# A hybrid attention and pooling layer on one core: the second layer norm, the forget logits, the loads of later heads and the output-weight splits, each put in another place

## The chip, the cores and the metric

The kernel runs on one core of a Trainium2 chip. The metric is device time in microseconds (us), the median of several runs. Five engines have a queue of their own and meet only through semaphores: PE (TensorE, matmuls), DVE (VectorE), ACT (ScalarE), POOL (GpSimd) and SP (SyncE). In this kernel SP issues every DMA.

## What is computed

One decoder layer on 2064 tokens (16 learned meta tokens ahead of 2048) of width 1024, in float32. Cut to what matters here:

```python
h = layer_norm(concat([meta, x]), ln_in_g, ln_in_b)
q, k, v, f_logit, g_att, u, g_pool = split(h @ w_in)        # 16 heads of 64
log_f = log_sigmoid(f_logit + b_forget); c = cumsum(log_f)
s = q.k / 8 + c_q - c_k                                     # causal
a = softmax(s) @ v * silu(g_att)
p = multiscale_pool(u) @ w_pool * pool_scale * silu(g_pool)
y = concat([a, p]) @ w_out
out = layer_norm(2 ** 0.25 * h + y, ln_g, ln_b)[:, 16:]
```

## The kernel before, in words

Every matrix operand is kept as two parts, a high part (`wh`, `hh`, `ph`: a copy rounded to the format that PE reads) and a low part (`wl`, `hl`, `pl`: the original less the high part). A product is then three matmuls (high x high, high x low, low x high; `mm3`, L107). `split` (L112) makes the parts: ACT copies, then DVE (or POOL) subtracts. A wrapper (L65 to L88) records every instruction and chains PE, DVE, ACT and POOL each to the order in which the code is written, so the trace gives L86 as the line of nearly everything, and tiles have to be told by name. SP is not chained: the tile scheduler places the DMAs.

The program has four stages.

1. **Input norm and values (0 to 232 us).** The tokens are worked in 17 tiles of 128 rows. `ln_norm(i)` (L227) takes the statistics of a tile's rows on DVE (`bn_stats`, `bn_aggr`), the root on ACT, the reciprocal and the shift on DVE, applies them on ACT, and multiplies by the gain `g_bc` and adds the shift `b_bc`, on the engines it is given (POOL by default). `ln_turn(i)` (L248) transposes the tile on PE (`tr`) and splits it into `hh` and `hl`. `v_tile(0, wts, i, each)` (L280) multiplies tile i by the first half of the value weights in eight steps of three matmuls, and calls `each(k)` after step k; the loop at L341 uses this to put `ln_turn(i + 1)` behind step 3 of tile i. The weights `wvh`, `wvl` of that half are split on ACT and DVE at L320 to L337, between the first norms. Then comes the second half of the values.
2. **Fused pool weights (232 to 262 us).** `fuse_mm(g)` (L418) multiplies the weights of the pool input by those of pool group g, for four groups: 48 matmuls of 256 columns each into two `fz` banks. `fuse_load`, `fuse_split` and `fuse_out` (L433 to L466) load and split a group's weights and write the result to DRAM (`wupd`). The code at L468 to L484 interleaves them. Then the forget logits (L507): five chunks of 16 matmuls into `d`, which has two banks; ACT copies one half of a chunk out (`zc`), DVE adds the other half, and a DMA writes it to `fd`.
3. **Projections (to 1316 us).** Queries and keys, gates and pool, with row maxima of the scores between them (`mx`).
4. **Attention and output (1316 us to the end).** The scores are worked in units: one key tile of 128 against a block of 512 queries, `(head, j)`, with 3, 7, 11 or 15 units in a block, so 36 to a head. A unit is two matmuls into `s` (four banks), two exponentials on ACT (`ph` and, in place, `s`), `pl = s - ph` on DVE (`emit_pl`), and, `LAG` = 4 units later, matmuls into `xo` and `yo`. The output projection runs as a filler: `fill(k)` puts up to four of its matmuls (`d<-wh,xm`) into a unit, from unit 24 on. Its weights come by `wo_task` (L941): `service()` (L1255), called in every second unit, is a round; each round first runs what is due (`todo_late`), then starts one load of 256 KB into `wst` (four buffers); the split of that load falls due three rounds later. There are three such sets of eight weights, at the start of attention, in the middle and near its end. `prefetch` (L888), called in every unit, takes the next group of 512 keys and values (`ka`, `kb`, `vt`) off a queue: any one group a call, and beyond that those that the current block or the next needs (`near`). Heads two apart share buffers, so a head's first group cannot be loaded before the head two before it is done. Phase C, the second norm of the output, follows.

Of the kernel before, what the change touches and what calls it, by code (L numbers as in the profile page):

```python
# [9 lines left out]
F32 = mybir.dt.float32  # L10
# [6 lines left out]
P = 128  # L17
# [18 lines left out]
def f32(ap):  # L36
    return ap.bitcast(F32)
# [3 lines left out]
def kernel(  # L41
# [59 lines left out]
    def dma(out, in_):  # L101
        out, in_ = out[tuple(slice(None) for _ in out.shape)], in_[tuple(slice(None) for _ in in_.shape)]
        nc.sync.dma_start(
            out.bitcast(F32) if out.dtype == F32R else out, in_.bitcast(F32) if in_.dtype == F32R else in_
        )
# [69 lines left out]
    def dense():  # L175
        return psd.tile([P, 512], F32, tag="d", name="d", bufs=2)
# [18 lines left out]
    with ExitStack() as vscope:  # L195
# [19 lines left out]
        def rows_of(i):  # L215
            return min(P, L - P * i)
# [7 lines left out]
            dma(xt[lo:n], x[P * i + lo - NM : P * i + n - NM, :])  # L224
            xts[i] = xt

        def ln_norm(i, engs=None):  # L227
            n = rows_of(i)
            xt = xts[i]
            st = lnp.tile([P, 2, 6], F32, tag="bst", name="bst", bufs=2)  # L230
            for k in range(2):
                nc.vector.bn_stats(out=st[:n, k, :], in_=xt[:n, 512 * k : 512 * (k + 1)])
            mv = lnp.tile([P, 2], F32, tag="mv", name="mv", bufs=2)
            nc.vector.bn_aggr(out=mv[:n], in_=st[:n])
            rs = lnp.tile([P, 1], F32, tag="rs", name="rs", bufs=2)
            nc.scalar.activation(out=rs[:n], in_=mv[:n, 1:2], func=AF.Sqrt, bias=eps_t[:n])
            nc.vector.reciprocal(rs[:n], rs[:n])
            nb = lnp.tile([P, 1], F32, tag="nb", name="nb", bufs=2)
            nc.vector.scalar_tensor_tensor(
                out=nb[:n], in0=mv[:n, 0:1], scalar=-1.0, in1=rs[:n], op0=ALU.mult, op1=ALU.mult  # L240
            )
            nc.scalar.activation(
                out=xt[:n], in_=xt[:n], func=AF.Identity, scale=rs[:n], bias=nb[:n]
            )
            for op, row, eng in zip((ALU.mult, ALU.add), (g_bc, b_bc), engs or (nc.gpsimd, nc.gpsimd)):
                eng.tensor_tensor(out=xt[:n], in0=xt[:n], in1=row[:n], op=op)

        def ln_turn(i):  # L248
            n = rows_of(i)
# [17 lines left out]
        def wv_split(st):  # L267
            h_, l_ = wslot("wvh"), wslot("wvl")
            split(h_, l_, st)
            return h_, l_  # L270
# [9 lines left out]
        def v_tile(half, wts, kt, each):  # L280
            ps = dense()
            sl = slice(P * kt, P * (kt + 1))
            for k in range(KT):
                mm3(ps, hh[:, k, sl], hl[:, k, sl], wts[k][0], wts[k][1], k == 0, k == KT - 1)
                each(k)
            v_out(half, kt, P, ps)
# [33 lines left out]
        def wv_hi(k):  # L320
            nc.scalar.copy(out=wts[k][0], in_=raw[k])
# [9 lines left out]
            wv_lo(k)  # L331
        ln_turn(0)
        ln_load(3)
        for k in range(2, KT):
            if k > 2:
                wv_hi(k)
            wv_lo(k)  # L337
        ln_norm(1, both)
        ln_norm(2, (nc.vector, nc.gpsimd))

        for i in range(NKT - 1):  # L341
            if 4 <= i + 4 < NKT:
                ln_load(i + 4)
            if i + 3 < NKT:
                ln_norm(i + 3)
            if i == 2:
                dma(wfs, wf)
                dma(bf_t, b_forget)
                dma(psc_t, pool_scale)
            if i == 5:  # L350
                split(wfr[:, :, 0:H], wfr[:, :, 32 : 32 + H], wfs)
            if i == 14:
                sts = deque(wv_load(1, k) for k in range(3))

            def turn(k, i=i):
                if k == 3:
                    ln_turn(i + 1)

            v_tile(0, wts, i, turn)
        w1 = [wv_split(sts.popleft())]  # L360
        lnscope.close()
        wq = pool(phase_a, "wq", side="right")
# [70 lines left out]
        def fuse_out(g, made):  # L433
            os = []
            for ps in made:
                os.append(raw4())
                nc.scalar.copy(out=os[-1], in_=ps)
            for half, o in enumerate(os):
                o = o.rearrange("p (k b e) -> p k b e", k=4, b=2)
                for b in range(2):  # L440
                    dma(wupd[2 * g + b][:, 4 * half : 4 * half + 4, :], o[:, :, b, :])
# [13 lines left out]
        def fuse_split(g, r):  # L455
            wst, st = r
            slots = []
            for k in range(2):
                if g % 2:
                    slots.append([fz.tile([P, D], F32R, tag=t, name=t, bufs=2) for t in ("uh", "ul")])  # L460
                else:
                    slots.append([flat(t) for t in w_slots()])
            us[g].append(u_split(st[0], slots[0]))
            wps[g] = [fz.tile([P, 2, 256], F32R, tag=t, name=t, bufs=2) for t in ("ph", "pl")]
            split(*wps[g], halves(wst))
            us[g].append(u_split(st[1], slots[1]))  # L466
# [5 lines left out]
        fuse_split(1, r)  # L472
        r = fuse_load(2)
        fuse_out(0, made)
        fuse_split(2, r)
        made = fuse_mm(1)
        r = fuse_load(3)
# [26 lines left out]
    )  # L504
    ones = fp.tile([P, 1], F32, tag="ones", name="ones")
    nc.vector.memset(ones, 1.0)
    for c0, c1 in CHUNKS:  # L507
        n = c1 - c0
        ps = dense()
        for k in range(KT):  # L510
            mm(ps[:48, :n], wfr[:, k, :], hh[:, k, c0:c1], start=k == 0, stop=False)
            mm(ps[:48, :n], wfr[:, k, :], hl[:, k, c0:c1], start=False, stop=k == KT - 1)
        zc = f32(qp.tile([P, 416], F32R, tag="lo", name="zc", bufs=2))[:H]
        nc.scalar.activation(
            out=zc[:, :n], in_=ps[32 : 32 + H, :n], func=AF.Identity, bias=bf_t
        )
        nc.vector.tensor_tensor(out=zc[:, :n], in0=ps[:H, :n], in1=zc[:, :n], op=ALU.add)
        dma(fd[:, c0:c1], zc[:, :n])
    FW = L // 8
    zf = fp.tile([P, FW], F32, tag="zf", name="zf")  # L520
    dma(zf, fd.rearrange("h (s t) -> (h s) t", s=8))
# [362 lines left out]
        kvq.extend((h, i) for i in range(4) if i <= j and (h, i) not in kvq)  # L884
    fetched = [0]
    cornered = [0]

    def prefetch(n, nv):  # L888

        k = 0  # L890
        while kvq:
            h, i = kvq[0]
            near = any(t[0] == h and t[1] >= i for t in seqn[n : n + 2])
            if h >= 2 and last_use[h - 2] >= nv or (k and not near) or first_use[h] > n + 5:
                break
            load_kv(h, i)
            kvq.popleft()
            k += 1
        while fetched[0] < min(NB, n + 3):
            load_q(fetched[0])  # L900
            fetched[0] += 1
        if cornered[0] < H and first_use[cornered[0]] <= n + 3:
            load_corner(cornered[0])
            cornered[0] += 1
# [36 lines left out]
    def wo_task(args):  # L941
        def a():
            st = wo_load(bw, *args)
            todo_late.append((state["round"] + 3, lambda: wo_split(bw, *args, st, None)))

        return a

# [505 lines left out]
```

## Time and profile before

| | |
|---|---|
| median of 3 runs | 2349.0 us (2347.35 to 2353.8) |
| the profiled execution | 2348.34 us, its span 2346.6 us |
| busy, share of the span | PE 97%, DVE 62%, ACT 42%, POOL 33% |
| DMA | 335.41 MB, mean 143 GB/s |

A profile's row of a timeline gives the start in us, the duration in us, the engine, the line, the operation, output<-inputs, and in brackets how long the engine had been idle and what it waited for. Rows of the chain of waits give start, duration and what the end of the program hung on then. A row of the windows gives, for a stretch of the span, its length and for each engine the busy time and the count of instructions, then the granted TensorE clock (1.00 is full speed) and the DMA share. A wait of PE costs time; a wait of another engine costs time only if PE comes to wait for it.

### The profile page before, as it was taken

How to read it: one execution, taken by the hardware profiler on the slowest of the kernel's cores; microseconds unless marked ns; L12 is line 12 of the kernel's file. 1: busy time of each engine (PE TensorE's matmuls, PEld its weight loads, DVE VectorE, ACT ScalarE, POOL GpSimd, SP SyncE). 2: the span in 40 equal slices, each digit the busy share in tenths (PEclk: the TensorE clock that was granted, in tenths of full speed). 3: DMA queues.
4: the chain of work that ended last, by engine and by line, in shares of the span. 5: the costliest groups of instructions: out<-in, count | busy, mean ns of one | idle time of the engine just before them, and what ended most of it. 6: DMA issues, size and time to landing. Idle time of an engine off the chain costs nothing.

```text
span 2346.6 us, 32233 instructions
## 1 busy us (share of the span) xinstructions
PE 2266.2 (97%) x11146; PEld 1902.4 (81%) x11146; DVE 1464.9 (62%) x2360; ACT 978.3 (42%) x1895; POOL 783.6 (33%) x624
## 2 busy tenths in 40 slices
PE   6999999999999999999999799999999999999998
PEld 4878799999999999999888577777777777776787
DVE  5521246755766567656634388787878777767347
ACT  4421421222212212211111387878878877776000
POOL 4700021222313404140010146555565655545000
PEclk9999999999999999999999899999999999999999
DMA  6743532222222222222222766675767767555955
GB/s 228 226 140 105 154 97 63 91 65 85 89 63 91 82 72 85 62 96 81 80 69 70 194 188 195 192 212 171 201 193 200 207 194 222 167 163 178 290 186 168
DMA packets 347778, 335.41 MB, mean 143 GB/s; under 512 B 57888, under 2 KB 271344, under 8 KB 347584
## 3 DMA queue, kind: packets, MB, share of 16 engines
q1 hardware_dynamic: 347616, 333.37, 47.0%
q8 instruction: 88, 1.44, 0.3%
q14 instruction: 74, 0.61, 0.1%
HBM read 209.15 MB, written 124.13 MB: 142 GB/s over the span
## 4 chain that ended last, share of the span: by engine, by line
PE 90%; DVE 3%; DMA 2%; issue 2%; ACT 2%; POOL 1%; SPq 0%; DVEq 0%; ACTq 0%; POOLq 0%
PE d L86 61%; PE s L86 11%; PE yo L86 7%; PE mx L86 6%; PE xo L86 5%; DVE pl L86 1%; PE fz L86 1%; PE tr L86 1%; DMA xm<-xa 1%; ACT ph L86 1%; DMA wst<-in_wout_dram 0%; SPq L86 0%; POOL acc L86 0%; ACT s L86 0%; POOL araw L86 0%
## 5 line engine op out<-in xcount | busy, mean ns | idle before, releaser
L86 PE MATMUL d<-hh,wh 128*128 128x412 f32 (+2 forms) x1472 | 543.6, 369 | 0.0
L86 PE MATMUL d<-hl,wh 128*128 128x412 f32 (+2 forms) x1472 | 538.3, 366 | 0.0
L86 PE MATMUL d<-hh,wl 128*128 128x412 f32 (+2 forms) x1472 | 537.9, 365 | 0.0
L86 DVE TENSOR_TENSOR pl<-s,ph 128x512 fp32r<-128x512 f32 (+3 forms) x592 | 373.5, 649 | 166.8 <-ACT s L86 158.2
L86 DVE TENSOR_REDUCE mxs<-mx 128x1 f32<-128x912 f32 (+14 forms) x416 | 359.5, 865 | 85.9 <-PE mx L86 76.1
L86 ACT ACTIVATE ph<-s 128x512 fp32r<-128x512 f32 (+3 forms) x592 | 336.9, 569 | 156.4 <-PE s L86 141.9
L86 PE MATMUL d<-wh,xm 128*128 128x512 f32 x1024 | 348.1, 397 | 4.2 <-DMA xm<-xa 3.4
L86 ACT ACTIVATE s<-s 128x512 f32<-128x512 f32 (+3 forms) x592 | 335.7, 567 | 0.0
L86 PEld LDWEIGHTS d<-hl,wh 128*128 128x128 f32 x1472 | 277.7, 189 | 24.8
L86 PEld LDWEIGHTS d<-hh,wh 128*128 128x128 f32 x1472 | 276.9, 188 | 23.0 <-ACT gst L86 0.3
L86 PEld LDWEIGHTS d<-hh,wl 128*128 128x128 f32 x1472 | 276.6, 188 | 23.3
L86 POOL TENSOR_TENSOR wl<-wst,wh 128x1024 fp32r<-128x1024 f32 x40 | 96.2, 2405 | 589.7 <-ACT wh L86 564.1
L86 PE MATMUL s<-qa,ka 68*128 68x512 f32 (+3 forms) x640 | 244.8, 383 | 21.5 <-DVE pl L86 21.1
L86 PE MATMUL yo<-pl,vt 128*66 128x512 f32 (+3 forms) x640 | 229.1, 374 | 11.3 <-ACT c L86 11.0
L86 PE MATMUL s<-qb,kb 128*128 128x512 f32 (+3 forms) x640 | 234.6, 367 | 0.0
L86 PE MATMUL xo<-ph,vt 128*128 128x512 f32 (+3 forms) x640 | 232.6, 367 | 0.0
L86 PEld LDWEIGHTS d<-wh,xm 128*128 128x128 f32 x1024 | 193.7, 190 | 47.1 <-issue 4.2
L86 POOL TENSOR_TENSOR tu<-ph 128x512 f32<-128x512 f32 x144 | 188.3, 1308 | 99.5 <-ACT ph L86 95.4
L86 PE MATMUL d<-wl,xm 128*128 128x512 f32 x512 | 203.1, 397 | 0.0
L86 PE MATMUL mx<-ka,qa 66*128 66x512 f32 (+5 forms) x704 | 198.2, 348 | 3.4 <-ACT qa L86 3.4
L86 PEld LDWEIGHTS s<-qa,ka 68*128 68x128 f32 x640 | 122.4, 191 | 61.4 <-DVE pl L86 33.7
L86 DVE TENSOR_TENSOR mx<-mx,mask_q 128x128 f32<-128x128 f32 x256 | 76.5, 299 | 117.8 <-PE mx L86 115.1
(185 smaller groups left out, 3097.4 us busy)
## 6 DMA issues: line engine op xcount, KB each, us to landing
xm<-xp SPq DMA_DIRECT2D x32, 1024.0 KB
xm<-xa SPq DMA_DIRECT2D x20, 1024.0 KB
vd<-vs SPq DMA_DIRECT2D x32, 512.0 KB
vt<-vd SPq DMA_DIRECT2D x64, 256.0 KB
qb<-kqd SPq DMA_DIRECT2D x64, 256.0 KB
xa<-am SPq DMA_DIRECT2D x32, 512.0 KB
xp<-pm SPq DMA_DIRECT2D x32, 412.0 KB
kqd<-lo SPq DMA_DIRECT2D x64, 206.0 KB
```

What stands on the lines that cost most here:

```text
L86: return in_order(f(*a, **k))
```

## The change

Four edits, all of order alone: the same instructions with the same sizes are issued.

1. Norm of tile 1. `ln_norm` is parted into `ln_stats` and `ln_apply`. The high parts of the value weights are made first on ACT, the statistics of tile 1 come after the low part of step 3 on DVE, two more low parts go between the statistics and the reciprocal, two more ahead of gain and shift. `ln_turn(1)` is put behind all eight steps of `v_tile(0, wts, 0)` instead of behind step 3, and the norms of tiles 2 and 3 behind that.
2. The forget logits stand between `fuse_out(0, ...)` and `fuse_split(2, ...)` instead of behind group 3, and their `zc` lies in the pool `fz`.
3. `prefetch` takes a group that isn't near only in every fifth call (`PACE`).
4. The split of an output weight falls due four rounds after its load, not three.

```diff
-        def ln_norm(i, engs=None):
+        def ln_stats(i, between=None):
...
             nc.scalar.activation(out=rs[:n], in_=mv[:n, 1:2], func=AF.Sqrt, bias=eps_t[:n])
+            if between:
+                between()
             nc.vector.reciprocal(rs[:n], rs[:n])
...
+        def ln_norm(i, engs=None):
+            ln_stats(i)
+            ln_apply(i, engs or (nc.gpsimd, nc.gpsimd))
...
-        for k in range(2, KT):
-            if k > 2:
-                wv_hi(k)
+        for k in range(3, KT):
+            wv_hi(k)
+        wv_lo(2)
+        wv_lo(3)
+
+        def lows():
+            wv_lo(4)
+            wv_lo(5)
+
+        ln_stats(1, lows)
+        for k in range(6, KT):
             wv_lo(k)
-        ln_norm(1, both)
-        ln_norm(2, (nc.vector, nc.gpsimd))
+        ln_apply(1, both)
 
         for i in range(NKT - 1):
             if 4 <= i + 4 < NKT:
                 ln_load(i + 4)
-            if i + 3 < NKT:
+            if 0 < i < NKT - 3:
                 ln_norm(i + 3)
...
             def turn(k, i=i):
-                if k == 3:
+                if k == 3 and i:
                     ln_turn(i + 1)
 
             v_tile(0, wts, i, turn)
+            if i == 0:
+                ln_turn(1)
+                ln_norm(2, (nc.vector, nc.gpsimd))
+                ln_norm(3)
...
         fuse_out(0, made)
+        for c0, c1 in CHUNKS:
+            n = c1 - c0
+            ps = dense()
+            for k in range(KT):
+                mm(ps[:48, :n], wfr[:, k, :], hh[:, k, c0:c1], start=k == 0, stop=False)
+                mm(ps[:48, :n], wfr[:, k, :], hl[:, k, c0:c1], start=False, stop=k == KT - 1)
+            zc = fz.tile([P, 416], F32, tag="zc", name="zc")[:H]
...
+            dma(fd[:, c0:c1], zc[:, :n])
         fuse_split(2, r)
...
+    PACE = 5
+    paced = [0]
 
     def prefetch(n, nv):
 
-        k = 0
+        paced[0] += 1
         while kvq:
...
-            if h >= 2 and last_use[h - 2] >= nv or (k and not near) or first_use[h] > n + 5:
+            if h >= 2 and last_use[h - 2] >= nv or (paced[0] < PACE and not near) or first_use[h] > n + 5:
                 break
             load_kv(h, i)
             kvq.popleft()
-            k += 1
+            paced[0] = 0
...
-            todo_late.append((state["round"] + 3, lambda: wo_split(bw, *args, st, None)))
+            todo_late.append((state["round"] + 4, lambda: wo_split(bw, *args, st, None)))
```

**The start.** On DVE, from the low part of weight step 2 on (`wvl` is a low part, `bst`, `mv`, `rs`, `nb` belong to the norm of tile 1):

```order
 L86 TENSOR_TENSOR wvl<-wraw,wvh 128x512
-L86 TENSOR_TENSOR wvl<-vs,wvh 128x512 x4
+L86 TENSOR_TENSOR wvl<-vs,wvh 128x512
+L86 BN_STATS bst<-xt 128x6 x2
+L86 BN_AGGR mv<-bst 128x2
+L86 TENSOR_TENSOR wvl<-vs,wvh 128x512 x2
+L86 RECIPROCAL rs<-rs 128x1
+L86 SCALAR_TENSOR_TENSOR nb<-mv,rs 128x1
+L86 TENSOR_TENSOR wvl<-vs,wvh 128x512
 L86 TENSOR_TENSOR wvl<-wst,wvh 128x512
-L86 BN_STATS bst<-xt 128x6 x2
-L86 BN_AGGR mv<-bst 128x2
```

The statistics of tile 1 moved ahead of four low parts. On ACT, a little later, from the application of tile 1's norm (`vs` is the first value tile's copy out of PSUM, `hh` the two high parts of the transposed tile 1; the `rs`, `xt` pairs are the norms of tiles 2 and 3):

```order
 L86 ACTIVATE xt<-xt,nb,rs 128x1024
+L86 CAST vs<-d 128x8x64
+L86 CAST hh<-tr 128x4x128 x2
 L86 ACTIVATE rs<-mv,eps_t 128x1
 L86 ACTIVATE xt<-xt,nb,rs 128x1024
 L86 ACTIVATE rs<-mv,eps_t 128x1
 L86 ACTIVATE xt<-xt,nb,rs 128x1024
-L86 CAST hh<-tr 128x4x128 x2
-L86 CAST vs<-d 128x8x64
```

The split of tile 1 moved ahead of the norms of tiles 2 and 3. On PE the eight transposes of tile 1 moved behind the last 12 of the 24 matmuls of the first value tile.

**The fuse groups.** On ACT, from the last high part of group 1 on (`raw<-fz` copies group 0 out, `zc` the logits, `wh` and `ph` are the high parts of group 2):

```order
 L86 CAST uh<-raw 128x1024
 L86 COPY raw<-fz 128x1024 x2
+L86 ACTIVATE zc<-d,bf_t 16x416
+L86 ACTIVATE zc<-d,bf_t 16x412 x4
 L86 CAST wh<-raw 128x1024
 L86 CAST ph<-wp 128x512
```

The five copies of logits moved ahead of group 2's splits; on DVE the five additions stand at the same place, and on PE the 80 matmuls of the logits stand between groups 0 and 1.

**The start of attention.** SP's queue before, around the third load of an output weight (`wst`; `ka`, `kb`, `vt` is one group of keys and values, `sd` a row sum on its way out):

```order
L86 DMA ka<-kqd 66x512
L86 DMA kb<-kqd 128x512
L86 DMA vt<-vd_58 128x4x128
L86 DMA wst<-in_wout_dram 128x512
L86 DMA ka<-kqd 66x512
L86 DMA kb<-kqd 128x512
L86 DMA vt<-vd_58 128x4x128
L86 DMA sd_81<-c_10589 1x512
L86 DMA ka<-kqd 66x512
L86 DMA kb<-kqd 128x512
L86 DMA vt<-vd_58 128x4x128
L86 DMA wst<-in_wout_dram 128x512 x2
```

And now, around the same load (`qa`, `qb` are a block's queries, `cqb` and `cv` belong to the first 16 tokens of the heads):

```order
L86 DMA cqb<-kqd 128x4x16
L86 DMA cv<-vd_58 16x128 x4
L86 DMA wst<-in_wout_dram 128x512
L86 DMA sd_81<-c_10577 1x512
L86 DMA wst<-in_wout_dram 128x512
L86 DMA ka<-kqd 66x512
L86 DMA kb<-kqd 128x512
L86 DMA vt<-vd_58 128x4x128
L86 DMA wst<-in_wout_dram 128x512
L86 DMA qa<-kqd 2x512
L86 DMA qa<-kqd 64x512
L86 DMA qb<-kqd 128x512
```

Between the first load of a weight and the third stood four groups of keys and values; now there is one, and the first two loads go out together.

More of the change, by code (lines that the diff above doesn't have):

```diff
@@ L244, in ln_norm, with ln_apply @@
             )
-            for op, row, eng in zip((ALU.mult, ALU.add), (g_bc, b_bc), engs or (nc.gpsimd, nc.gpsimd)):
+        def ln_apply(i, engs):
+            n = rows_of(i)
+            xt = xts[i]
+            for op, row, eng in zip((ALU.mult, ALU.add), (g_bc, b_bc), engs):
                 eng.tensor_tensor(out=xt[:n], in0=xt[:n], in1=row[:n], op=op)
+        def ln_norm(i, engs=None):
+            ln_stats(i)
+            ln_apply(i, engs or (nc.gpsimd, nc.gpsimd))
         def ln_turn(i):
@@ L474 @@
         fuse_out(0, made)
+        for c0, c1 in CHUNKS:
[5 more added lines that the diff above has]
+            zc = fz.tile([P, 416], F32, tag="zc", name="zc")[:H]
+            nc.scalar.activation(
+                out=zc[:, :n], in_=ps[32 : 32 + H, :n], func=AF.Identity, bias=bf_t
+            )
+            nc.vector.tensor_tensor(out=zc[:, :n], in0=ps[:H, :n], in1=zc[:, :n], op=ALU.add)
+            dma(fd[:, c0:c1], zc[:, :n])
         fuse_split(2, r)
@@ L506 @@
     nc.vector.memset(ones, 1.0)
[L507 to L518, printed above, removed]
     FW = L // 8
```

## The prediction

> **What bounds the kernel now.** I read the page first, then PE's waits by stage, the windows around each, the chain, and the timelines of the engines named there. PE is the bound: it is busy for 97% of the span below, and in the long middle its waits are short.
>
> ```profile
> span 2346.6 us, 32233 instructions
> PE 2266.2 (97%) x11146; PEld 1902.4 (81%) x11146; DVE 1464.9 (62%) x2360; ACT 978.3 (42%) x1895; POOL 783.6 (33%) x624
> ```
>
> The change issues the same matmuls, so it can only gain or lose where PE stands idle or runs at a reduced clock. Four PE rows carry the long waits at the places that it touches (the brackets hold the idle time and what ended it).
>
> ```profile
> 24.61 1.94 PE L86 MATMUL tr<-ident,xt 128*128 128x128 f32 x8 [7.55 <-DVE xt L86]
> ...
> 33.47 0.50 PE L86 MATMUL d<-wvh,hh 128*128 128x512 f32 x1 [3.24 <-ACT hh L86]
> ...
> 242.77 0.58 PE L86 MATMUL fz<-ph,uh 128*128 128x256 f32 x1 [4.70 <-ACT raw L86]
> ...
> 1348.78 0.69 PE L86 MATMUL yo<-pl,vt 128*66 128x512 f32 x1 [9.95 <-ACT c L86]
> ```
>
> Together 25.4 us. Each is followed by matmuls at half clock, as the windows show (the number behind the five engines is the granted clock).
>
> ```profile
> 24.60:30.30 5.70, 5.63 (x20) 4.52 (x20) 3.90 (x8) 1.53 (x2) 1.00 (x1) 0.67 0.52 184
> 238.00:243.00 5.00, 0.30 (x2) 0.23 (x2) 3.05 (x3) 2.96 (x4) 0.00 (x0) 0.70 0.93 335
> 243.00:248.00 5.00, 5.00 (x28) 5.00 (x29) 2.97 (x3) 3.31 (x5) 0.00 (x0) 0.61 0.89 248
> 248.00:262.00 14.00, 14.00 (x119) 13.97 (x118) 3.00 (x4) 8.16 (x9) 2.44 (x2) 1.00 0.91 276
> 1338.80:1348.80 10.00, 0.05 (x2) 0.02 (x1) 3.31 (x5) 4.79 (x10) 2.27 (x2) 0.69 0.96 263
> 1348.80:1353.00 4.20, 4.20 (x11) 3.08 (x12) 3.36 (x6) 3.39 (x7) 2.19 (x3) 0.53 0.65 180
> ```
>
> At full clock a `fz` matmul takes 14.00 / 119 = 0.118 us; after the wait at 242.77 it is 5.00 / 28 = 0.179 us. So a long wait costs itself and some 2 us behind it.
>
> **Edit 1, the start.** Rows of DVE, PE, POOL and ACT, in order of time:
>
> ```profile
> 15.42 2.49 DVE L86 TENSOR_TENSOR wvl<-vs,wvh 128x512 fp32r<-128x512 f32 x4
> ...
> 18.43 1.28 DVE L86 BATCH_NORM_STATS2 bst<-xt 128x6 f32<-128x512 f32 x2
> ...
> 20.70 1.24 ACT L86 ACTIVATE xt<-xt,nb,rs 128x1024 f32<-128x1024 f32 x1 [0.42 <-DVE nb L86]
> ...
> 23.24 1.23 DVE L86 TENSOR_TENSOR xt<-xt,b_bc 128x1024 f32<-128x1024 f32 x1
> 24.38 1.28 DVE L86 BATCH_NORM_STATS2 bst<-xt 128x6 f32<-128x512 f32 x2
> ...
> 29.30 2.36 POOL L86 TENSOR_TENSOR xt<-xt,b_bc 128x1024 f32<-128x1024 f32 x1 [26.48 <-DVE xt L86]
> ...
> 32.86 1.05 ACT L86 CAST hh<-tr 128x512 fp32r<-128x512 f32 x2
> ...
> 37.78 1.46 PE L86 MATMUL tr<-ident,xt 128*128 128x128 f32 x8
> ```
>
> Before, tile 1's norm runs from 18.43 to 24.47 while PE stands. Now its statistics begin after one low part, at 15.42 + 2.49 / 4 = 16.0. From there to the application on ACT it was 20.70 - 18.43 = 2.3 us; the two low parts put between add 2 x 0.62, less a few tenths in which DVE had to wait for ACT's root anyway. ACT applies from about 19.2 to 20.5, gain and shift follow at 1.23 us each, and the transposes start at about 23.0 instead of 24.6. Meanwhile PE does the other 12 matmuls of tile 0, held to the pace of the low parts, until about 21.
>
> Before, tile 1's transposes were done at 26.6, but its high parts waited on ACT behind two norms until 32.86. Now they come directly, about 24.1 (1.1 us after the first transpose), and tile 1's matmuls start at about 24.8 instead of 33.5. That isn't kept: after step 3 they need tile 2, whose norm now follows tile 1's low parts on DVE, at 26.3 (from 24.1, two casts of 0.5 and two subtractions of 0.6). From its statistics to the shift on POOL took 29.30 + 2.36 - 24.38 = 7.3 us, so tile 2 is transposed at 33.6 instead of 37.8. The new late thing is thus tile 2's norm: PE stands from 27.6 (12 matmuls at 0.23) or 29.4 (at 0.38) until 33.6. Of the 4.2 us I take 2.0 back, for 12 matmuls at half clock (0.38 us by the last window, 4.20 / 11, against 0.23 us in the row below) after that wait: a gain of 2.2, between 0.5 and 4.0. From there PE sets the pace as before, a tile in 24 x 0.232:
>
> ```profile
> 39.24 5.56 PE d L86 x24
> ```
>
> The Trainium skill, TensorE: Matmul & The Clock Gate, Part 1 (the HAM clock gate), says that PE falls to half rate after an idle window of about 3.4 us and returns after a busy one of that length, with windows that run freely. The windows above agree; by that rule the new wait leaves all 12 matmuls at half rate, 12 x 0.232 = 2.8 us more, and edit 1 gives an estimated 1.4 us in place of 2.2.
>
> **Edit 2, the forget logits.** Before, PE waits 4.70 us for group 1's splits, runs three groups, then the logits. Two rows of the chain, then rows of ACT, DVE and POOL:
>
> ```profile
> 236.20 4.41 DMA raw<-in_wut_dram
> 242.77 19.24 PE fz L86 x144
> ```
>
> ```profile
> 241.70 1.93 ACT L86 COPY raw<-fz 128x1024 f32<-128x1024 f32 x2
> ...
> 257.36 1.05 ACT L86 CAST wh<-wst 128x1024 fp32r<-128x1024 f32 x1
> ...
> 258.48 2.40 POOL L86 TENSOR_TENSOR wl<-wst,wh 128x1024 fp32r<-128x1024 f32 x1 [133.90 <-ACT wh L86]
> ...
> 265.08 0.60 ACT L86 ACTIVATE zc<-d,bf_t 16x416 f32<-16x416 f32 x1 [2.02 <-PE d L86]
> ...
> 265.71 0.58 DVE L86 TENSOR_TENSOR zc<-d,zc 16x416 f32<-16x416 f32 x1 [3.69 <-ACT zc L86]
> ...
> 277.01 0.60 ACT L86 ACTIVATE zc<-d,bf_t 16x412 f32<-16x412 f32 x1 [2.38 <-PE d L86]
> ```
>
> A chunk takes (277.01 - 265.08) / 4 = 2.98 us. Their operands have long been there, so PE goes from group 0 (end 238.1) straight into chunks 0 and 1, until 244.0. Chunk 2 needs chunk 0's bank: ACT frees itself at 241.70 + 1.93 = 243.6, copy and addition take 0.60 + 0.58, so 244.8: a new wait of 0.8. Chunks 2 to 4 end at 253.8, group 1 at 259.5. Behind the last chunk ACT makes two `wh` (1.05 each) and a `ph` (half that) of group 2, DVE subtracts, and that is done near 259, in time by half a us. At the end the first gate weight's low part on POOL came 260.88 - 262.01, about 1.1 us, ahead of its use, and keeps that distance.
>
> So the wait of 4.70 goes, the half clock goes (19.24 - 144 x 0.118 = 2.3), 0.8 comes: 6.2 us. Below, 3.9 if the clock drops anyway; above, 7.0 without the new wait.
>
> **Edits 3 and 4, the start of attention.** ACT's two rows are the splits of the third and fourth output weight; the chain's last two rows are their loads, its first one issue on SP.
>
> ```profile
> 1340.44 0.62 ACT L86 CAST wh<-wst 128x512 fp32r<-128x512 f32 x1 [5.74 <-DMA wst<-in_wout_dram]
> ...
> 1346.62 0.62 ACT L86 CAST wh<-wst 128x512 fp32r<-128x512 f32 x1 [3.57 <-DMA wst<-in_wout_dram]
> ```
>
> ```profile
> 1325.88 0.43 SPq L86
> ...
> 1334.96 5.46 DMA wst<-in_wout_dram
> 1340.43 6.16 DMA wst<-in_wout_dram
> ```
>
> PE's 9.95 us is ACT blocked by casts whose data weren't there: 5.74 + 3.57 = 9.3 us. The third load was issued only at 1334.96, behind keys of heads 0 and 1, and DMA was busy at 0.96. Now SP has one group of keys ahead of that load where there were four: nine issues fewer, at 0.43 us and the waits between them, put it at 1330 to 1331. By the longer landing, 6.2 us, it is there at 1336 to 1337. Its cast was due at 1340.44 - 5.74 = 1334.7 and now comes a round, two units or about 2 us of exponentials, later: 1336.7, just in time. The fourth load follows the third at once and has a round more. Both waits go, and since ACT sets the pace before the filler starts in unit 24, its 9.3 us return, with about 0.7 from PE's half clock: 10.0 us, between 7 (a late third load) and 11.7 (9.95 + 11 x (0.38 - 0.23)). The last split falls in unit 23, so the filler starts no later.
>
> The later load has a cost: with four buffers and four rounds, each further load waits on SP for DVE's subtraction of the one four before it, and what is queued behind on SP are queries and keys needed a block later. At the two later sets the splits, and so the next set of filler, come two units later; in those PE lacks filler and ACT is the longer:
>
> ```profile
> L86 ACT ACTIVATE ph<-s 128x512 fp32r<-128x512 f32 (+3 forms) x592 | 336.9, 569 | 156.4 <-PE s L86 141.9
> ```
>
> Two exponentials of 0.57 and half a cast of 0.62 against four matmuls of 0.232 are at most 0.5 us a unit, 2.0 us for two units in two sets; exponentials overlap, so I take half, 1.0. What falls beside what on DVE changes too:
>
> ```profile
> L86 DVE TENSOR_TENSOR wl<-wst,wh x32: 673/684/1761, 1331.6 to 2209.8; 128x512 fp32r<-128x512 f32 x32
> ...
> 2139.51 0.80 PE L86 MATMUL s<-qa,ka 68*128 68x512 f32 x1 [3.66 <-DVE pl L86]
> ```
>
> The second row's wait lies in the last set; it may shrink or grow. So the 1.0 lies between a gain of 1 and a loss of 3. Elsewhere in attention the slower loading of keys hides nothing that PE waits for, and gives nothing.
>
> **Sum.** 2.2 + 6.2 + 10.0 - 1.0 = 17.4 us. The profiled execution took 2348.3, so 2330.9; the median lies 0.7 above it: 2331.6.
>
> **Rivals.**
>
> *The wait moves on (11%).* The first two casts of attention find their data, but loads five to eight now wait for subtractions and their casts are late in turn. For: SP serves one queue. Against: a load has eight units. If half of the 10.0 stays, 2336.6.
>
> *Start or fuse groups gain little (5%).* PE's wait only changes place (27.6 to 33.6) and the logits make group 2 late: without edit 1 and with 3.9 for edit 2, 2336.1.
>
> *Collisions (8%).* The row of `wl` above spans 673 to 1761 ns; the long cases I take for subtractions that POOL holds up. If in the two later sets all 16 subtractions were long ones, 16 x (1761 - 684) = 17.2 us, and the time is 2349, no change. Against: PE holds four `s` banks, and most such delays never reach it. The Trainium skill, SBUF — State Buffer, § Who interferes with whom, says that a DVE instruction with two SBUF inputs contends with a GpSimd one that reads SBUF; the row's spread agrees.
>
> *Late keys, slower (4%).* Pacing turns loads that stood ready into loads that a head waits for. A head's four groups now take 20 of the 36 units of the head before it; should they come one landing late,
>
> ```profile
> 1326.36 4.95 DMA vt<-vd
> ```
>
> 14 heads x 4.95 = 69 us, and the time is 2401. It decides from 17.4 / 14 = 1.2 us a head. Against: a group that the next block needs is loaded at once, pace or not.
>
> **How the numbers follow.** The forecast has 72%. The bounds of its terms (0.5 + 3.9 + 7 - 3, and 4.0 + 7.0 + 11.7 + 1) add up to 8.4 to 23.7 us of gain; the ends together are unlikely, so 9 to 23, and the first two rivals lie inside: 2326 to 2340, about 8 in 10. About 0.3%, 7 us, is what a measurement of this kernel can tell from no change. Faster by more: 72 + 11 + 5 = 88%; within: 8%; slower: 4%.
>
> **What would show it.** Right: PE's transposes of tile 1 near 23 and of tile 2 near 33.6; logits from 238 to 254 with one short gap and no half clock; no cast of `wst` that waits in attention, PE without a wait over 3 us between 1325 and 1362 (shifted). Wrong: a PE wait of 5 us or more for `wh` or `fz`, a split of group 2 that ends last, PE waits on `ka`, `kb` or `vt` at the first units of a head, or a sum of PE's waits in attention as large as before.

## The result and the profile after

The changed kernel takes 2337.5 us in the median of six runs (2334.2 to 2340.0); the kernel before, on the same chip, lies between 2347.35 and 2353.8, a disturbed run of 5709 us left out. The ratio is 0.9946, with an interval of 0.9933 to 0.9960: about 12 us faster, where 17.4 were forecast. On another chip, later, it was 2339.4 against 2347.2 (ratio 0.9964, 0.9951 to 0.9977): 7.8 us, which is less than the 9 at the low end of the gains that the prediction counted on. The profiled execution took 2337.55 us.

The page of the changed kernel, its span and its engines:

```profile
span 2335.5 us, 32223 instructions
...
PE 2267.7 (97%) x11146; PEld 1900.4 (81%) x11146; DVE 1467.1 (63%) x2360; ACT 978.4 (42%) x1895; POOL 784.1 (34%) x624
```

The same matmuls, 1.5 us more of PE's busy time and a span 11.1 us shorter: PE stands less. To see where, the span is cut at rows of PE that both traces have. In the changed kernel they are these, in order: the wait for the last tokens' `hs`, the first matmul for row maxima that waits, the first score of attention that waits, a score behind its start, and a wait for `c` ahead of the last output tiles.

```profile
133.93 0.40 PE L86 MATMUL d<-wvh,hs 128*48 128x512 f32 x1 [2.23 <-DVE hs L86]
...
432.01 0.33 PE L86 MATMUL mx<-ka,qa 66*128 66x144 f32 x1 [0.59 <-ACT qa L86]
...
1314.97 0.50 PE L86 MATMUL s<-qa,ka 68*128 68x512 f32 x1 [0.85 <-DVE pl L86]
...
1416.33 0.45 PE L86 MATMUL s<-qa,ka 68*128 68x400 f32 x1 [0.71 <-DVE pl L86]
...
2081.76 0.45 PE L86 MATMUL yo<-ph,zo 128*66 128x512 f32 x1 [1.16 <-ACT c L86]
```

| stretch | holds | before, us | after, us | after - before | forecast |
|---|---|---|---|---|---|
| start, to `hs` | edit 1 | 135.88 | 133.93 | -1.95 | -2.2 |
| to `mx` | edit 2 | 300.55 | 298.08 | -2.47 | -6.2 |
| to the first `s` | projections | 882.98 | 882.96 | -0.02 | 0 |
| to `s` near 1416 | edits 3 and 4, first weights | 109.32 | 101.36 | -7.96 | -10.0 |
| to `c` near 2081 | middle of attention | 666.89 | 665.43 | -1.46 | 0 |
| to the end | last weights, tail | 250.98 | 253.74 | +2.76 | +1.0 (two sets) |

The sum is -11.1. Now the waits in those stretches. PE's rows at the four places that the prediction started from:

```profile
22.78 1.86 PE L86 MATMUL tr<-ident,xt 128*128 128x128 f32 x8 [1.86 <-DVE xt L86]
...
33.17 1.97 PE L86 MATMUL tr<-ident,xt 128*128 128x128 f32 x8 [4.84 <-POOL xt L86]
...
242.91 0.39 PE L86 MATMUL d<-hh,wfr 128*48 128x412 f32 x1 [0.76 <-DVE zc L86]
...
247.52 0.40 PE L86 MATMUL d<-hh,wfr 128*48 128x412 f32 x1 [1.42 <-DVE zc L86]
...
252.21 0.39 PE L86 MATMUL d<-hh,wfr 128*48 128x412 f32 x1 [1.50 <-DVE zc L86]
...
1334.43 0.45 PE L86 MATMUL yo<-pl,vt 128*66 128x512 f32 x1 [0.82 <-ACT c L86]
...
1347.03 0.62 PE L86 MATMUL s<-qa,ka 68*128 68x512 f32 x1 [1.89 <-DVE pl L86]
```

The transposes start where they were expected (23.0 and 33.6 in the prediction), behind 1.86 and 4.84 us of waiting. The wait of 4.70 for group 1's splits is gone, but three waits for a `d` bank stand in its place where one of 0.8 was forecast: 3.7 us. The 9.95 for `c` has become 0.82, and there is a wait of 1.89 that was not there before. The windows around these places, of the changed kernel:

```profile
22.70:28.40 5.70, 5.55 (x20) 4.26 (x20) 3.64 (x8) 1.68 (x4) 0.00 (x0) 0.70 0.60 199
33.10:38.60 5.50, 5.43 (x20) 4.41 (x20) 3.28 (x6) 3.23 (x5) 4.05 (x3) 0.69 0.53 176
...
243.00:248.00 5.00, 3.58 (x19) 2.12 (x20) 0.58 (x1) 0.60 (x1) 0.00 (x0) 1.00 0.98 285
248.00:262.00 14.00, 12.50 (x88) 10.35 (x87) 4.69 (x6) 6.00 (x8) 0.00 (x0) 1.00 0.27 96
1338.80:1345.00 6.20, 5.70 (x28) 3.67 (x27) 6.13 (x11) 6.20 (x15) 3.03 (x3) 1.00 0.96 269
1345.00:1351.00 6.00, 4.12 (x15) 3.10 (x15) 5.94 (x9) 3.28 (x8) 2.52 (x2) 0.72 0.97 286
2147.00:2153.00 6.00, 4.13 (x11) 3.14 (x11) 1.96 (x3) 0.90 (x2) 0.22 (x1) 0.72 0.80 247
```

The half clock around the forget logits is gone as forecast (1.00). From 1338.80 to 1345.00 ACT is busy for all of 6.20 us and DVE for 6.13: behind the stall that went, the work of both fills the time. The last row belongs to the tail, where the change loses. There, PE's first matmul of the last set's output tiles and its three waits:

```profile
2138.46 0.44 PE L86 MATMUL d<-wh,xm 128*128 128x512 f32 x1
...
2149.08 0.56 PE L86 MATMUL d<-wh,xm 128*128 128x512 f32 x1 [1.87 <-DVE yt L86]
2157.19 0.50 PE L86 MATMUL d<-wh,xm 128*128 128x512 f32 x1 [0.78 <-DVE yt L86]
2163.71 0.50 PE L86 MATMUL d<-wh,xm 128*128 128x512 f32 x1 [0.78 <-DVE yt L86]
```

And the same in the kernel before, with one wait:

```profile
2149.78 0.40 PE L86 MATMUL d<-wh,xm 128*128 128x512 f32 x1
...
2167.55 0.50 PE L86 MATMUL d<-wh,xm 128*128 128x512 f32 x1 [0.78 <-DVE yt L86]
```

`d` has a single bank in attention, so each output tile's first matmul waits until DVE has read the tile before it (`yt`); while scores run, that hides behind them. In the changed kernel the first `d` of the last set starts at 2138.5, with the last score, at 2138.8; before it started at 2149.8, 5 us ahead of the last score, at 2154.8. The half clock behind the wait of 1.87 (0.72 in the last window) belongs to this execution: four other traces below have the same wait, of 1.87 or 1.88 us, and 1.00 over the 6 us from its beginning on.

So three questions were open: what makes the three `zc` waits, which edit removed the 9.95, and whether edit 4 is what lengthens the tail.

### The profile page after: what moved, and what is told of

Its sections match the earlier page's. It is cut to its first block, busy times and chain, and to the rows that moved or that the text cites. A ratio compares the mean times of both kernels' runs of the same rounds, so it can differ in the third digit from the quotient of the medians.

```text
span 2335.5 us, 32223 instructions
## 1 busy us (share of the span) xinstructions
PE 2267.7 (97%) x11146; PEld 1900.4 (81%) x11146; DVE 1467.1 (63%) x2360; ACT 978.4 (42%) x1895; POOL 784.1 (34%) x624
## 4 chain that ended last, share of the span: by engine, by line
PE 90%; DVE 3%; ACT 3%; issue 2%; DMA 1%; POOL 0%; SPq 0%; DVEq 0%; ACTq 0%; POOLq 0%
PE d L86 60%; PE s L86 11%; PE yo L86 7%; PE mx L86 6%; PE xo L86 5%; DVE pl L86 1%; ACT ph L86 1%; PE fz L86 1%; PE tr L86 1%; ACT s L86 1%; DVE yt L86 0%; DMA xm<-xa 0%; DMA b_bc<-in_ln_in_b_dram 0%; DVE bst L86 0%; DMA fd<-zc 0%
```

## The experiments

Each run's profiled trace was cut at the same five rows. The projections came out at 882.9 to 883.3 us in every one. The other stretches vary more between kernels that are the same there: the start by 0.8 us, the stretch to `mx` by up to 2.5, the start of attention by up to 1.8, the middle by up to 3.3 and the end by up to 3.4; so single rows are weak, and the means over several traces carry the argument. The times are medians, with the kernel before, run beside them, behind the stroke; their intervals are some 3 us wide either way, and edits 1 and 2 alone are hardly told from no change by them (ratios 0.9991, 0.9981 to 1.0, and 0.9993, 0.9984 to 1.0003). "At three rounds" means the splits of the output weights.

| kernel | time / before | start | to `mx` | att. start | middle | end |
|---|---|---|---|---|---|---|
| edit 1 alone | 2345.6 / 2347.4 | 133.50 | 301.00 | 108.39 | 666.27 | 250.13 |
| edit 2 alone | 2345.7 / 2347.4 | 135.88 | 297.73 | 108.94 | 666.54 | 251.16 |
| edit 3 alone | 2340.8 / 2347.4 | 135.06 | 302.10 | 101.75 | 665.52 | 249.12 |
| edit 4 alone | 2344.4 / 2347.4 | 135.52 | 302.18 | 106.60 | 667.28 | 253.41 |
| changed, again | 2339.4 / 2347.2 | 133.52 | 299.85 | 101.65 | 665.85 | 254.12 |
| two places for `zc` | 2334.0 / 2347.1 | 133.14 | 295.67 | 100.09 | 663.67 | 252.37 |
| last set at three rounds | 2333.1 / 2347.1 | 133.25 | 299.53 | 101.65 | 666.38 | 251.79 |
| all sets at three rounds | 2334.6 / 2347.1 | 133.20 | 299.35 | 101.72 | 666.95 | 251.54 |
| tile 2's shift on DVE | 2339.0 / 2347.1 | 134.25 | 297.33 | 101.77 | 664.76 | 253.72 |
| filler two turns sooner | 2333.2 / 2347.2 | 133.70 | 299.63 | 101.87 | 665.31 | 251.95 |
| two `zc`, all at three | 2331.5 / 2347.2 | 133.51 | 294.51 | 101.85 | 665.89 | 251.60 |
| two `zc`, last set at three | 2332.7 / 2347.2 | 133.37 | 296.05 | 101.52 | 664.27 | 252.47 |

### Each edit alone

Edit 1 alone: the hunks of `ln_stats`, `ln_apply` and the loop; its core is

```diff
-                if k == 3:
+                if k == 3 and i:
                     ln_turn(i + 1)
...
+            if i == 0:
+                ln_turn(1)
+                ln_norm(2, (nc.vector, nc.gpsimd))
+                ln_norm(3)
```

> The kernel before with edit 1 alone (norm of tile 1, turn of tile 1, norms of tiles 2 and 3). Theory: tile 2's norm is the new late thing. PE waits 1.9 us for tile 1's xt near 22.8 and 4.8 for tile 2's near 33.2, where before it waited 7.55 and 3.24, and all behind is 1.9 us earlier: PE's wait for the remainder of the tokens (hs), at 135.88 before, comes at 133.9, and the span is 2344.7. Rival: edit 1 gains more by itself and the other edits take some back through DMA; then hs comes before 133.0.

Measured: waits of 1.85 and 5.12 us, `hs` at 133.50. Over all runs the start takes 135.6 without the edit (mean of four) and 133.5 with it (nine, the kernel with tile 2's shift on DVE left out): 2.1 us. The theory stands.

Edit 2 alone: the logits' loop moved, with `zc` from the pool `fz`.

```diff
-        zc = f32(qp.tile([P, 416], F32R, tag="lo", name="zc", bufs=2))[:H]
...
+            zc = fz.tile([P, 416], F32, tag="zc", name="zc")[:H]
```

> The kernel before with edit 2 alone (forget logits between the fuse groups). Theory: the one buffer of zc makes ACT wait some 4 us for the DMA of the chunk before, so PE waits three times for a d bank between 244 and 255, 3.7 us in all; PE's wait for the first row maxima (mx), at 435.84 before, comes 2.5 us earlier, and the span is 2344.1. Rival: the three waits came from edit 1's shift of the DMAs; then there is one wait of 0.8 and the gain is 5 to 6 us, span 2341.

Measured: three waits of PE for `zc`, 1.00, 1.28 and 0.99 us, and a gain of 2.8 us to `mx`. Three waits stand there without edit 1, so the rival falls.

Edit 3 alone:

```diff
-        k = 0
+        paced[0] += 1
...
-            if h >= 2 and last_use[h - 2] >= nv or (k and not near) or first_use[h] > n + 5:
+            if h >= 2 and last_use[h - 2] >= nv or (paced[0] < PACE and not near) or first_use[h] > n + 5:
...
-            k += 1
+            paced[0] = 0
```

> The kernel before with edit 3 alone (PACE 5, splits still three rounds after the load). Theory: pacing alone brings the third output weight in time, since its load is issued 10 to 11 us after the first scores instead of 16; its cast waits under 0.5 us, PE's wait of 9.95 goes and the start of attention gains 7 to 8 us; with splits three rounds later as before the tail loses nothing, so the span is 2337 to 2339. Rival: both edits are needed, the third and fourth casts each still wait 2 us or more, and the gain is 3 to 5 us: span 2342 to 2344.

Edit 4 alone:

```diff
-            todo_late.append((state["round"] + 3, lambda: wo_split(bw, *args, st, None)))
+            todo_late.append((state["round"] + 4, lambda: wo_split(bw, *args, st, None)))
```

> The kernel before with edit 4 alone (splits four rounds after the load, keys as before). Theory: the third load is still issued near 1335 and lands near 1340.4, and its cast falls due 2 us later, so ACT still waits some 6 to 7 us for the two casts and PE's wait of 9.95 shrinks by 2 to 4; and the tail, where the splits of the last set come two units later, loses 2 to 3 us by bare waits for yt after the last scores. Span 2345 to 2348. Rival: the round alone does it and the tail is unharmed: PE's wait is gone, the span 2337 to 2339.

With edit 3 alone the start of attention takes 101.75 us, as good as with both. The timeline of SP has the third load, of ACT its cast, both of the kernel with edit 3 alone:

```profile
1330.62 0.42 SPq L86 DMA_DIRECT2D wst<-in_wout_dram  x1
```

```profile
1335.60 0.63 ACT L86 CAST wh<-wst 128x512 fp32r<-128x512 f32 x1
```

Its first score that waits ran at 1320.4, so the load is issued 10.2 us behind it (before: 1334.96 - 1319.41 = 15.6), and the cast, three rounds later, has no wait. With edit 4 alone ACT still waits twice, and PE for it (the timelines of ACT and of PE of that kernel):

```profile
1342.73 0.62 ACT L86 CAST wh<-wst 128x512 fp32r<-128x512 f32 x1 [4.48 <-DMA wst<-in_wout_dram]
...
1348.36 0.62 ACT L86 CAST wh<-wst 128x512 fp32r<-128x512 f32 x1 [2.56 <-DMA wst<-in_wout_dram]
```

```profile
1344.89 0.69 PE L86 MATMUL yo<-pl,vt 128*66 128x512 f32 x1 [5.41 <-ACT c L86]
```

Both theories held in the main; PE's wait shrank by 4.5 us with edit 4 alone, where 2 to 4 were expected, and that profiled execution was the slowest of its ten (2349.7, the median 2344.4). Pacing alone gives 7.1 us (101.8 against 108.9 in the mean), the later split alone 2.3, both 7.5: what the later split adds here, 0.4, is less than the stretch varies by itself. And the end stretch is long, 253.41, with edit 4 alone, and not with edit 3 alone, 249.12.

### Parts of the changed kernel undone

Two places for `zc`, in different partitions of one tile:

```diff
+        zt = fz.tile([P, 416], F32, tag="zc", name="zc")
...
-            zc = fz.tile([P, 416], F32, tag="zc", name="zc")[:H]
+            zc = zt[64 * (ci % 2) : 64 * (ci % 2) + H]
```

(`ci` counts the chunks.)

> The changed kernel with the zc of odd chunks in another half of the same tile (partitions 64 to 79), so that a chunk's copy waits for the transfer of the chunk two before, not of the one before. Theory: the single zc made the three waits of PE (3.7 us); they shrink to under 1.5 us in all, PE's first wait for row maxima (mx), at 431.4 in the changed kernel, comes 2 to 3 us earlier and the span is 2332.5 to 2333.5. Rival: each transfer to fd takes so long that two places don't help, or ACT's turn sets it; then the waits keep over 3 us and nothing moves.

ACT's copies in the changed kernel, and, with two places, those of the last three chunks (the brackets end on what the copy waited for):

```profile
246.26 0.60 ACT L86 ACTIVATE zc<-d,bf_t 16x412 f32<-16x412 f32 x1 [4.02 <-DMA fd<-zc]
250.95 0.60 ACT L86 ACTIVATE zc<-d,bf_t 16x412 f32<-16x412 f32 x1 [4.09 <-DMA fd<-zc]
253.79 0.60 ACT L86 ACTIVATE zc<-d,bf_t 16x412 f32<-16x412 f32 x1 [2.24 <-DMA fd<-zc]
256.64 0.60 ACT L86 ACTIVATE zc<-d,bf_t 16x412 f32<-16x412 f32 x1 [2.25 <-DMA fd<-zc]
```

```profile
246.24 0.60 ACT L86 ACTIVATE zc<-d,bf_t 16x412 f32<-16x412 f32 x1 [3.28 <-PE d L86]
249.22 0.60 ACT L86 ACTIVATE zc<-d,bf_t 16x412 f32<-16x412 f32 x1 [2.39 <-PE d L86]
252.20 0.60 ACT L86 ACTIVATE zc<-d,bf_t 16x412 f32<-16x412 f32 x1 [2.38 <-PE d L86]
```

With one place every copy behind the first waits for the transfer of the chunk before it; with two, ACT waits only for PE, and the logits run at PE's pace, 2.98 us a chunk. (In the last of the kernels below one copy still waits for a transfer, 3.55 us, but no wait of PE follows from it.) PE is left with one wait:

```profile
243.00 0.39 PE L86 MATMUL d<-hh,wfr 128*48 128x412 f32 x1 [1.65 <-DVE zc L86]
```

The stretch to `mx` takes 301.5 us without edit 2 (mean of four), 298.8 with one place (seven), 295.4 with two (three): the gain of edit 2 is 2.7 with one place and 6.1 with two. The remaining wait was expected under 1.5 and came at 1.65 here, at 0.48 and 0.44 in the two kernels below; it is the one that the prediction forecast at 0.8, and that the changed kernel has at 0.76.

The last set at three rounds:

```diff
-            todo_late.append((state["round"] + 4, lambda: ...
+            todo_late.append((state["round"] + (4 if args[0] else 3), lambda: ...
```

> The changed kernel with the splits of the last set of output weights three rounds after the load again, those of the first two sets four. Theory: the later splits of the last set let the filler start too late, so that after the last scores there are four output tiles to do instead of three and PE waits for yt three times instead of once; undone, the last set starts some 4 to 5 us ahead of the last scores, the stretch from PE's wait for c near 2113 to the end falls from 222.3 to 219 or 220 us, and the span is 2332 to 2333.5. Rival: the tail was longer for another reason (pacing, alignment of the blocks); then the stretch stays within 0.7 of 222.3.

All sets at three rounds, edit 4 taken back:

> The changed kernel without edit 4, all splits three rounds after the load (edits 1 to 3 are left). Theory: pacing alone removed PE's wait of 9.95 us, so the start of attention (first wait for s to the wait pair before 1416, 101.5 us in the changed kernel, 109.4 before) is at most 0.6 longer, and the tail is shorter as in the run with the last set alone: span 2332 to 2334, so edit 4 costs 2 to 3 us on the whole. Rival: in this context the third cast is due before its load lands, since the attention starts earlier than the loads do; then its cast waits 1 us or more and PE waits 2 us or more for c, and the span is 2335 or over.

The filler of the last set two turns sooner, with the splits left at four rounds (`out_tiles`):

```diff
-        for _ in range(3 if half else 5):
+        for _ in range(3):
             yield 0
```

> The changed kernel, all splits four rounds after the load, but the filler of the last set starts two turns sooner (it lets three turns pass behind the last split instead of five). Theory: what costs is that the filler starts behind the last scores; with it the first output tile of the last set stands ahead of the last four units again, only one wait for yt is left bare, and the stretch from the wait for c near 2081 to the end falls from 254.9 to 252 to 253.3 us, as with the earlier split. Rival: the late splits themselves cost, by ACT and DVE work beside the last scores; then PE waits for wh or wl at the start of that filler, or the stretch stays at 254 or over.

This kernel and the two at the end ran on another chip, so the changed kernel ran there once more:

> The changed kernel itself once more, as the measure for the other three on the same chip. All theories: 2335 to 2339 us, some 0.994 to 0.9955 of before; the stretch from PE's wait for c near 2081 to the end 253.5 to 255 us.

It took 2339.4 us, 0.9964 of before, both just above what was expected. The end stretch, counted from the wait's beginning as in that text, was 255.3; from the row's start, as in the table, it is 254.1.

The end stretch is 251.8, 251.5 and 252.0 in the three, against 253.7 and 254.1 in the changed kernel. In each of them one wait for `yt` is left. Of the kernel with the sooner filler, whose splits are as late as in the changed one, PE's rows behind the last scores, and the window that holds the first wait for `yt` in the changed kernel:

```profile
2156.17 0.50 PE L86 MATMUL d<-wh,xm 128*128 128x512 f32 x1 [0.78 <-DVE yt L86]
2164.36 0.47 PE L86 MATMUL d<-wh,xm 128*128 128x512 f32 x1 [2.44 <-DMA xm<-xa]
```

```profile
2147.00:2153.00 6.00, 6.00 (x32) 4.94 (x31) 2.40 (x4) 2.14 (x4) 1.22 (x2) 1.00 0.55 183
```

(The wait of 2.44 is for the transfer of `xm`; every trace has such a wait there, 2.12 before and 2.03 in the changed kernel.) PE is busy for all of the window. So it is the late start of the filler that costs, not the splits' work. It costs some 2 us: over all runs the end takes 253.5 with edit 4 untouched (five) against 251.1 with three rounds at the end (eight), 2.4 us. The changed kernel's two traces have 253.9 against 251.8 in these three. With two places for `zc` the difference is only 0.3 (252.4 in a single trace, against 252.0 in the two kernels at the end), within what the stretch varies by itself. The half clock is no part of it: of the five traces with a wait of 1.87 or 1.88 us for `yt` only the first of the changed kernel has it.

Without edit 4 at all the start of attention is 101.72, against 101.36 and 101.65 with it: the rival, a third cast that waits in this context, falls. The profiled spans, 2335.8 with the last set at three rounds and 2335.9 with all, were over what was expected (2332 to 2334), and that of two places for `zc`, 2327.9, under it (2332.5). The former two are the slowest of their four executions, the latter the fastest; the medians in the table are nearer to what was expected. The middle took 666.4 and 667.0 us in the former and 663.7 in the latter; why it varies by 3 us between runs isn't settled.

Tile 2's shift on DVE:

```diff
-                ln_norm(2, (nc.vector, nc.gpsimd))
+                ln_norm(2, both)
```

> The changed kernel with the shift of tile 2's norm on DVE instead of POOL. Theory: tile 2's norm is what PE now waits for at the start (4.84 us, ended by POOL's addition of 2.34); DVE does it in 1.23, so the transposes of tile 2 start near 32.0 instead of 33.17 and the wait for hs comes 0.7 to 1.1 us earlier, at 132.8 to 133.2. Rival: DVE's later norm of tile 3 becomes the late thing and takes it back; then PE waits 0.5 us or more for tile 3 between 38 and 48 and hs stays at 133.9.

PE's rows of that kernel:

```profile
31.16 1.94 PE L86 MATMUL tr<-ident,xt 128*128 128x128 f32 x8 [4.05 <-DVE xt L86]
38.76 0.50 PE L86 MATMUL d<-wvh,hh 128*128 128x512 f32 x1 [1.09 <-ACT hh L86]
```

Tile 2's transposes start 31.16 - 22.48 = 8.7 us behind tile 1's instead of 33.17 - 22.78 = 10.4, so its norm was what PE waited for. But 1.09 us come back as a wait for tile 3, and `hs` is at 134.25, 0.8 behind the mean: the rival, and slightly worse. The theory named the right wait; shortening it gains nothing.

### Both repairs together

> Edits 1 to 3 with two places for zc and all splits three rounds after the load (edit 4 taken back). Theory: both repairs add up, 2.4 to 2.9 from zc and 1.5 to 2.5 from the tail, less some 0.5 at the start of attention: 4 to 5 us under the changed kernel on the same chip, near 2332 to 2333. Rival: they don't add, since the shorter start only moves where the half-clock windows fall; then 2334 to 2335.

> The changed kernel with two places for zc, and the splits of the last set alone three rounds after the load. Theory: 4 to 5 us under the changed kernel on the same chip, and at most 1 us under the kernel with all splits at three rounds, whose third and fourth output weights were already nearly in time: 2332 to 2333. Rival: as there, 2334 to 2335.

Two places for `zc` with edit 4 taken back: 2331.5 us (2329.5 to 2336.1), ratio to before 0.9934 (0.9919 to 0.9949). With the last set alone at three rounds: 2332.7 (2331.2 to 2333.1), 0.9934 (0.9918 to 0.9951). The changed kernel on the same chip took 2339.4 (2337.0 to 2340.6). Against that run the profiled spans are 7.7 and 7.0 us shorter, of which 5.3 and 3.8 lie in the stretch to `mx` and 2.5 and 1.7 in the end stretch: more than the 4 to 5 expected. Against the changed kernel's first result (0.9946) the gain is only 0.0012 of before, 2.8 us, and the last set alone at three rounds has the same ratio of 0.9934. So that the repairs add is borne out by where the time went, in the two stretches, but not shown by the times. The two kernels are not told apart either.

## Why the prediction was right, and where it was wrong

The median fell in the range, 6 us above the value named. In the pair of traces edit 2 gave 3.7 us less than forecast, the start of attention 2.0 less, and the last weights cost 1.8 more; 1.5 us came back in the middle, which was not forecast and so was luck.

**Edit 1: right.** 2.2 forecast, 1.95 in the pair of traces and 2.1 in the means. Both transposes came within half a microsecond of their forecast, and tile 2's norm is the new late thing. The two windows at the start granted 0.70 and 0.69; with half and full clock as the only speeds that is 5.70 x 0.30 / 0.5 = 3.4 us and 5.50 x 0.31 / 0.5 = 3.4 us at half clock. The Trainium skill, TensorE: Matmul & The Clock Gate, Part 1 (the HAM clock gate), gives the window as about 3.4 us, and these agree, though the first of them came behind a wait of only 1.86 us; the prediction's estimate of 1.4 us by that rule, with all 12 matmuls at half rate, was farther off than 2.2. (The 2.0 taken back in the prediction is 1.8 by its own figures, 12 x (0.38 - 0.23), and the bound of 11.7 for the start of attention is 11.6; neither changes the account.)

**Edit 2: the step that failed.** "A new wait of 0.8" was worked out from the two `d` banks and ACT's time alone. It left out `zc` itself, which has two buffers in the kernel before; the diff shows that it has one in `fz`, with a DMA as its reader (so the edit is not of order alone: it also takes a buffer away). The wait of 4.70 went and the half clock with it, as the step says, but three waits came where one was counted: 3.7 us in the changed kernel instead of 0.8. The first, 0.76, is the one that was counted; the single `zc` makes the other two. With two places the gain is 6.1 against 6.2 forecast, so the rest of the step was right. Group 2 was in time, even behind an ACT that was held until 257.1.

**Edits 3 and 4: right in kind, 2.5 us too large** (10.0 forecast, 7.5 in the means). No cast waits and the 9.95 is gone. Shown by the runs: pacing alone does it; the later split, "a round more" in the prediction, was not needed. Too large was "its 9.3 us return", since "ACT sets the pace" left out DVE: PE's waits in this stretch fell from 15.0 us to 7.1, by 7.9, and among those left are a new 1.89 and 0.50 behind DVE's `pl`. Nor did the 0.7 for the half clock return in this trace, since the new wait of 1.89 brings one too (0.72). DVE is as full there as ACT (6.13 and 6.20 of 6.20 us, above), and it is DVE that PE waits for: ACT had finished the exponential that this `pl` needs at 1342.54, almost 4 us before DVE came to it. Ahead of it in DVE's queue a subtraction of `tl` took 1.66 us, beside an addition of POOL:

```profile
1341.98 0.56 ACT L86 ACTIVATE s<-s 128x416 f32<-128x416 f32 x1
...
1344.65 1.27 POOL L86 TENSOR_TENSOR acc<-ph 128x512 f32<-128x512 f32 x1 [3.17 <-ACT ph L86]
...
1344.81 1.66 DVE L86 TENSOR_TENSOR tl<-acc,th 128x512 fp32r<-128x512 f32 x1
...
1346.40 0.58 DVE L86 TENSOR_TENSOR pl<-s,ph 128x416 fp32r<-128x416 f32 x1
```

The subtraction takes 0.69 as a rule (shortest, median and longest of the 48 in the changed kernel, in ns), so about 1.0 of the 1.89 us is the long one, by an estimate from these rows:

```profile
L86 DVE TENSOR_TENSOR tl<-acc,th x48: 691/693/1822, 1329.8 to 2142.6; 128x512 fp32r<-128x512 f32 x48
```

**The cost at the later sets: mis-sized, and of another kind.** Forecast was 1.0 over two sets, from ACT being the longer engine while PE lacks filler. The middle set shows no loss (its stretch is 1.5 us shorter in the pair, 1.3 in the means of ten runs with edit 3 and four without; what gains there isn't settled). The last set alone costs about 2 us, by waits for `yt` that lie bare once the scores are over; the 2.76 of the pair has a half clock besides, which the other traces do not show. That end was within the bounds (a loss of up to 3).

**The rivals.** The wait did not move on to loads five to eight. The slower loading of keys made no head wait: PE waits for `ka`, `kb` or `vt` nowhere in attention. Collisions of DVE and POOL are there, as the rows above and below show, but nowhere near 17 us of them: from the first wait of attention to the end the span is 6.7 us shorter. Of the rival by which start and fuse groups gain little, the half on edit 2 came true: 2.5 to 2.8 us is less than the 3.9 that it reckoned with.

## What to carry to other kernels

When code is moved to another pool, read the number of buffers there: a tile with one buffer whose reader is a DMA ties its writer to the whole transfer, and here that gave back over half of the gain. A step that delays work by two units costs nothing where other work covers it, and its full price where it is the last: look at each place that shares the constant, the end of the program above all, and test such edits one at a time, since here one of two that came together (the later split) cost some 2 us at the end and, beside the other, gave next to nothing at the start. And when a long stall goes, price what was hidden behind it on every engine that feeds PE, not only on the one that stalled.

## What the runs showed of the hardware

A wait of PE of some 2 us brings the half clock in some executions and not in others. Behind waits of 1.89 and 1.87 us the windows from 1345 and from 2147 granted 0.72, which is 6.00 x 0.28 / 0.5 = 3.4 us at half clock each. But four other traces have the wait of 1.87 or 1.88 for `yt`, and there the 6 us from its beginning on were granted 1.00. The wait of 2.23 us for `hs` stands in all 14 traces; the 5 us behind it were granted 0.66 in seven of them and 1.00 in the other seven. Three waits of 0.76 to 1.50, with 3 us of matmuls between them, left the clock at 1.00. So the length of a wait alone does not decide; what does is not shown here. Where a half clock of 3.4 us comes, it costs an estimated 1.7 us beside the wait. It can last longer: behind the wait of 3.77 us for tile 2 in the second trace of the changed kernel it was 0.50 over all of 5.50 us.

A transfer of 16 x 412 numbers (26 KB) held its buffer longer among larger ones: ACT's waits for it were 4.02 and 4.09 us while the DMA share was 0.96, and 2.24 and 2.25 where it was 0.05. Each holds DVE's addition, some 0.6 us, and the first also 0.4 us in which SP was still issuing other transfers.

A DVE instruction of 128 x 1 numbers can take ten times its time beside POOL. Rows of DVE and POOL in the changed kernel:

```profile
34.49 2.37 POOL L86 TENSOR_TENSOR xt<-xt,g_bc 128x1024 f32<-128x1024 f32 x1 [1.37 <-ACT xt L86]
...
34.99 0.16 DVE L86 RECIPROCAL rs<-rs 128x1 f32<-128x1 f32 x1 [0.42 <-ACT rs L86]
35.19 1.68 DVE L86 SCALAR_TENSOR_TENSOR nb<-mv,rs 128x1 f32<-128x1 f32 x1
```

The shift `nb`, with two inputs in SBUF, ends at 36.87, with POOL's instruction at 36.86; the reciprocal, with one input, runs beside POOL in its usual 0.16. This agrees with the rule of the Trainium skill that the prediction cites (SBUF — State Buffer, § Who interferes with whom), and shows that the price here was the rest of POOL's instruction, however small DVE's is. It repeats: the longest `nb` takes 1.67 to 1.70 us in all ten traces with edit 1, and at most 0.50 in the four without.
